# Head norms of two token tiles taken together in a decoder layer's projection, with new numbers in its planner

## The chip, the cores and the metric

The kernel runs on one core of a Trainium2 chip. The metric is the device time of one execution in microseconds (us), taken as the median of the runs shown. One execution was also recorded by the profiler. TensorE (PE in the profile; its weight loads are PEld) multiplies matrices and transposes, VectorE (DVE) and ScalarE (ACT) do elementwise work, and SyncE (SP) issues nearly all DMAs. A matmul writes into PSUM, which is handed out here as banks of 128 x 512 floats.

## The reference, cut to what matters

One layer of a decoder trunk: a half-step SwiGLU feed-forward, an RMS norm, one wide projection `u @ W_in`, three attentions, a gated merge through `W_out`, and a second half-step feed-forward. 1024 tokens, model width 1024, all in float32.

```python
h = x + 0.5 * swiglu(rmsnorm(x, g1), ...)
u = rmsnorm(h, g)
z = u @ W_in                      # fox q,k,v,f | dsa q,k,v | indexer q,k,w | mem q | gates
fq, fk = head_norm(fq), head_norm(fk)      # 8 heads of 64, RMS over each head, then gains
dq     = rope(head_norm(dq))               # 8 heads of 64
o_A = fox_attention(...)          # causal, with log forget gates
o_B = dsa_attention(...)          # each query keeps the top 256 keys by indexer scores
o_C = memory_attention(...)       # 4 heads of 128 over 256 memory tokens
h = h + (sum_i sigmoid(u @ W_g_i) * (o_i @ W_br_i)) @ W_out
y = h + 0.5 * swiglu(rmsnorm(h, g2), ...)
```

(The lines on the three norms of heads stand here in short for what the kernel computes between the projection and the attentions; the two other score products, the masks and the softmaxes are left out.)

## The kernel before, in words

Every large product is made of three TensorE products of split operands (`mm3`): each float32 operand is held as a high part and a rest, and high by high, high by rest and rest by high are summed in PSUM. ACT makes the high part of a weight (`wH`), DVE the rest (`wL`). Tokens come in 8 tiles of 128.

The program runs in this order: feed-forward 1 (to about 690 us), norm and the narrow columns of the projection, the wide columns of the projection (about 735 to 1108 us), the attentions (to 1698), the last branch product and the product with `W_out`, feed-forward 2.

**The projection.** Six column blocks of 512 run one after the other over the 8 tiles, in the order MQ (memory queries), IQ (indexer queries), FK and FQ (keys and queries of the forgetting attention), FV (its values), DQ (queries of the sparse attention). `Block.step` is one tile of one block: 24 matmuls of 512 columns into one PSUM bank, `tm`, then a `consume` of its own. For MQ, FK, FQ and DQ this is `head_norm`: ACT squares the bank into a tile in SBUF (`hsq`), DVE sums it by heads (`hv`), nine small DVE operations on 128 x 8 values make the reciprocal root (`rs_y`, `rs_a`), and one DVE multiplication writes the normed tile. For DQ a rotation follows (five DVE operations). Then `turn` transposes the tile on PE through another bank, ACT and DVE split it (`th`, `tl`), and SP stores both parts. FV's consume is one split and one store; it has no norm and no turn.

In this stage PSUM is four single banks, shared by `tm`, `turn` and the gate products, and two buffers of two banks each (`banks2`), which the index scores `isc` use. An index score is four matmuls of up to 512 columns into such a double bank (fewer columns for earlier tiles), a ReLU on ACT and a weighted sum on DVE (`acc`). As soon as a tile of queries has its scores, `selection`, a background chain, looks for the threshold of its top 256 keys by bisection, 32 rounds for a tile: ACT counts over the score row (`junk`), DVE makes the next threshold (`sk`, `sn`).

**The planner.** `_Flow` writes the order out when the program is built. It keeps a clock for each engine from a small table of costs; chains of work are generators that yield between steps, each with a time (`c.t`) at which its next step is ready. `fl.run(chains, width, filler, background, pace)` takes the first ready chain of the first `width`, else a step of `filler`, and steps `background` whenever it is due. The compiler's scheduler then orders the instructions of each engine on that basis. In the projection the filler is the gate product (`gates_f`, 96 steps of 12 matmuls); what is left of it, then branch products 2 and 0 (16 steps of 12 each, named `br`), is the filler of the attentions. There `pace()` lets the filler run as far as the heads' share of their steps, plus `PACE` steps, and holds `RESERVE` steps back; `left` (L1751) is the number of filler steps that the heads spread out. Branch 1 has to wait for the last sparse head: `last_branch` stores that head's output, loads it again with the others' (`wS<-o_s`), splits it (`wH` and `wL` in the profile) and runs 192 matmuls.

**The start of the attentions.** `mem_head` issues four loads on SP (`qs`, `vs`, `km`, `vm`), says when its operands are expected (`fl.t = max(fl.t, fl.clk["PE"]) + 4.0`, L1267) and yields; its first matmuls are `spm`. Two heads are open at a time (`width=2`). On SP these loads stand behind the last stores of the sparse queries.

Of the kernel before, what the change touches and what calls it, by code (L numbers as in the profile page):

```python
# [9 lines left out]
F32 = mybir.dt.float32  # L10
# [9 lines left out]
P = 128  # L20
# [132 lines left out]
PACE, RESERVE = 4, 6  # L153


def trunk_layer_kernel(
# [182 lines left out]
    class Block:  # L339
# [13 lines left out]
        def step(self, u, t, consume, after=None):  # L353
# [5 lines left out]
            pt = self.out(t) if self.out else bank("tm")  # L359
            kper = 1024 // self.ncols  # L360
# [7 lines left out]
            yield from consume(t, pt)  # L368
# [8 lines left out]
    def block_chains(blocks, u, nt, deps=None, after=None):  # L377
        cs = []
        for i, (b, consume) in enumerate(blocks):
            nxt = blocks[i + 1][0] if i + 1 < len(blocks) else after  # L380
            order = getattr(consume, "order", range(getattr(consume, "first", 0), nt))
            for t in order:
                cs.append(chain(b.step(u, t, consume, nxt if t == order[-1] else None),
                                deps[t] if deps and i == 0 else getattr(consume, "deps", ())))
# [472 lines left out]
    def head_norm(tp, pt, nh, sq=None):  # L857
        hd = 512 // nh
# [397 lines left out]
    def mem_head(tp, h):  # L1256
# [10 lines left out]
        fl.t = max(fl.t, fl.clk["PE"]) + 4.0  # L1267
# [379 lines left out]
    def normed(dst, nh, scale):  # L1647
        def consume(t, pt):
            xn = head_norm(tp, pt, nh)
            yield  # L1650
            parts = turn(tp, xn, scale)
            if nh == 8:
                store_pairs(dst, t, parts)
            else:
                for i, w in enumerate(parts):
                    store(dst[i].rearrange("h d t -> d h t")[:, :, t * P:(t + 1) * P], w)
        return consume

    def sparse_queries(t, pt):
        xn = head_norm(tp, pt, 8)  # L1660
        o = tp.tile([P, 512], F32, tag="hx", name="hsq", bufs=4)
        bc = lambda a, s: a.unsqueeze(1).to_broadcast(s)
        rotate(tp, o.rearrange("p (h a d) -> p h a d", h=8, a=2), xn.rearrange("p (h a d) -> p h a d", h=8, a=2),
               bc(cgq[:, t], [P, 8, 2, 32]), bc(sgq[:, t, 0], [P, 8, 32]), bc(sgq[:, t, 1], [P, 8, 32]), 8)
        yield
        store_pairs(dq_s, t, turn(tp, o))

    def fox_values(t, pt):
# [6 lines left out]
    blocks = [(mq_block, normed(mq_s, 4, gmx[:, 0:1])), (mk_block(C_IQ), index_queries),  # L1675
              (mk_block(C_FK), normed(fk_s, 8, None)), (mk_block(C_FQ), normed(fq_s, 8, gfx[:, 0:1])),
              (mk_block(C_FV), fox_values), (mk_block(C_DQ), sparse_queries)]
# [73 lines left out]
    left = 2 * 24 * 2 - gates_f.n + 40  # L1751
# [121 lines left out]
```

## Time and profile before

| | us |
|---|---|
| median of 3 runs | 2497.53 |
| fastest and slowest run | 2496.92 and 2503.78 |
| the profiled execution | 2504.25 |
| its span, first to last instruction | 2502.2 |
| PE busy in that span | 2412.6 (96%) |
| DVE and ACT busy | 1617.9 (65%) and 1149.1 (46%) |
| mean granted TensorE clock | 0.984 of full speed |

The busy shares are means over stages with different limits, so the profile is read stage by stage: a table of windows gives the length of a stage, each engine's busy time in it and the clock that TensorE was granted; the table of waits says what an idle PE waited for; the timeline shows single instructions with the idle time before them; and the chain of waits shows what led to the work that ended last.

### The profile page before, as it was taken

The page shows a single profiled execution, that of the slowest core. Times are in us where ns is not written, and L with a number is a line of the kernel's source. Part 1 is how long each engine was busy: PE and PEld are TensorE (multiplying, and loading weights), DVE is VectorE, ACT ScalarE, POOL GpSimd, SP SyncE. Part 2 cuts the span into 40 slices and gives each one's busy share as a digit, 9 for nine tenths or more (in the row PEclk, how much of TensorE's full clock was granted, in tenths as well). Part 3 has the DMA queues.
Part 4 walks back from the last instruction along what each step waited for, and adds up shares of the span by engine and source line. Part 5 has one row for each costly group of instructions (what it writes and reads, how often), then busy time and mean ns, then how long its engine had stood idle before and what let it go on. Part 6 is the DMA issues. An engine that isn't in the chain of part 4 may idle for free.

```text
span 2502.2 us, 31494 instructions
## 1 busy us (share of the span) xinstructions
PE 2412.6 (96%) x11532; PEld 1995.0 (80%) x11532; DVE 1617.9 (65%) x3162; ACT 1149.1 (46%) x1918; POOL 2.2 (0%) x40
## 2 busy tenths in 40 slices
PE   6999999999999999989999999998999999999999
PEld 5888888888788877777787888887877888888887
DVE  7755555478767588685564556777367555554885
ACT  6443333343443376768864555543144333333332
POOL 0000000000000000000000000000000000000000
PEclk8999999999999999999999999999999999999999
DMA  4333322484445534544554546667413222225643
GB/s 136 117 103 110 101 92 73 146 316 142 135 131 146 163 100 137 164 147 137 153 162 135 154 133 195 194 200 238 145 64 93 85 93 76 84 93 194 260 151 131
DMA packets 300922, 352.15 MB, mean 141 GB/s; under 512 B 19896, under 2 KB 202840, under 8 KB 300768
## 3 DMA queue, kind: packets, MB, share of 16 engines
q1 hardware_dynamic: 300768, 350.15, 43.7%
q8 instruction: 90, 1.47, 0.2%
q14 instruction: 64, 0.52, 0.1%
HBM read 255.51 MB, written 93.54 MB: 139 GB/s over the span
## 4 chain that ended last, share of the span: by engine, by line
PE 74%; DVE 12%; ACT 7%; DMA 4%; issue 3%; SPq 0%; ACTq 0%; DVEq 0%
PE gx L51 19%; PE gy L51 14%; PE dx L51 8%; PE gate L51 7%; PE tm L51 7%; PE dy L51 6%; PE br L51 4%; ACT junk L51 3%; PE po L51 2%; PE sp L51 2%; DVE wL L51 2%; PE pT L51 2%; DMA wS<-in_ffn_w_down 1%; PE nar L51 1%; ACT ns L51 1%
## 5 line engine op out<-in xcount | busy, mean ns | idle before, releaser
L51 ACT CAST wH<-wS 128x1024 fp32r<-128x1024 f32 (+1 forms) x218 | 204.6, 944 | 260.7 <-PE gy L51 78.0
L51 PE MATMUL tm<-wH,u 128*128 128x512 f32 x992 | 319.5, 396 | 3.4 <-ACT wH L51 3.4
L51 DVE TENSOR_TENSOR wL<-wS,wH 128x1024 fp32r<-128x1024 f32 (+1 forms) x218 | 236.2, 1089 | 101.1 <-ACT wH L51 98.8
L51 PE MATMUL gate<-u,wH 128*128 128x512 f32 x768 | 248.9, 401 | 0.0
L51 PE MATMUL gx<-th,wH 128*128 128x512 f32 x704 | 223.2, 399 | 10.3 <-ACT wH L51 6.2
L51 PE MATMUL gy<-th,wH 128*128 128x512 f32 x704 | 220.9, 395 | 5.3 <-DVE th L51 3.5
L51 PEld LDWEIGHTS tm<-wH,u 128*128 128x128 f32 x992 | 187.4, 189 | 42.0 <-ACT wH L51 4.6
L51 PE MATMUL gx<-raw,wH 128*128 128x512 f32 x704 | 216.9, 389 | 0.4 <-DVE gu L51 0.4
L51 PE MATMUL tm<-wL,u 128*128 128x512 f32 x496 | 195.1, 393 | 1.0 <-DVE wL L51 0.8
L51 ACT ACTIVATE junk<-wk,sn 128x384 bf16<-128x384 f32 (+5 forms) x186 | 164.3, 883 | 67.4 <-DVE sn L51 59.0
L51 PEld LDWEIGHTS gx<-th,wH 128*128 128x128 f32 x704 | 135.0, 193 | 40.6 <-ACT wH L51 7.4
L51 ACT CAST wH<-S 128x1024 fp32r<-128x1024 f32 x88 | 92.2, 1051 | 157.9 <-PE gy L51 149.9
L51 PEld LDWEIGHTS gy<-th,wH 128*128 128x128 f32 x704 | 133.6, 190 | 34.7 <-DVE th L51 4.4
L51 PEld LDWEIGHTS gate<-u,wH 128*128 128x128 f32 x768 | 140.3, 191 | 24.8 <-DVE u L51 0.2
L51 DVE TENSOR_TENSOR pl<-pT,ph 128x512 fp32r<-128x512 f32 (+1 forms) x176 | 110.1, 639 | 74.5 <-ACT ph L51 73.1
L51 DVE TENSOR_TENSOR wL<-S,wH 128x1024 fp32r<-128x1024 f32 x88 | 107.4, 1223 | 75.1 <-ACT wH L51 75.1
L51 DVE TENSOR_TENSOR gu<-gu,gy 128x512 f32<-128x512 f32 x88 | 60.3, 686 | 147.0 <-PE gy L51 104.1
L51 PEld LDWEIGHTS gx<-raw,wH 128*128 128x128 f32 x704 | 132.0, 188 | 28.2 <-DVE gu L51 0.8
L51 PE MATMUL gate<-u,wL 128*128 128x512 f32 x384 | 151.7, 395 | 0.0
L51 PE MATMUL dx<-wH 128*128 128x512 f32 x352 | 138.4, 393 | 2.7 <-DVE rows L51 2.6
L51 PE MATMUL gx<-th,wL 128*128 128x512 f32 x352 | 139.1, 396 | 0.6 <-DVE wL L51 0.5
L51 PE MATMUL gy<-th,wL 128*128 128x512 f32 x352 | 138.8, 394 | 0.0
(270 smaller groups left out, 5018.1 us busy)
## 6 DMA issues: line engine op xcount, KB each, us to landing
wS<-in_ffn_w_down SPq DMA_DIRECT2D x70, 512.0 KB
wS<-in_w_in SPq DMA_DIRECT2D x48, 512.0 KB
wS<-in_ffn_w_gate SPq DMA_DIRECT2D x46, 512.0 KB
wS<-in_ffn_w_up SPq DMA_DIRECT2D x44, 512.0 KB
hid_s<-gu SPq DMA_DIRECT2D x44, 512.0 KB
a<-hid_s SPq DMA_DIRECT2D x30, 512.0 KB
g_s<-sg SPq DMA_DIRECT2D x48, 256.0 KB
bg<-g_s SPq DMA_DIRECT2D x48, 256.0 KB
```

What stands on the lines that cost most here:

```text
L51: return fn(*a, **k)
```

## The change

Four edits.

1. The norm of heads for FK, FQ and DQ takes two tiles at once. `Block.pair` makes both tiles' products (2 x 24 matmuls) into the two halves of one double bank, from the same two buffers that the index scores use, and `pair_norm` runs one norm over 128 x 1024. Turns, rotations and stores stay one for each tile. MQ keeps its norm of one tile.
2. FV moves from fifth place to third: MQ, IQ, FV, FK, FQ, DQ.
3. `PACE` goes from 4 to 8, and the constant in `left` from 40 to 37: the filler may run 8 steps ahead of the heads, and 3 steps more of it are kept for after them.
4. Memory heads 0 and 1 expect their operands 12.0 instead of 4.0 after PE's clock.

```diff
-PACE, RESERVE = 4, 6
+PACE, RESERVE = 8, 6
...
+        def pair(self, u, t, consume, after=None):
+            self.fetch()
+            if fl.clk["PE"] < self.ready[0]:
+                yield self.ready[0]
+            pt = banks2("tm")
+            self.product(pt[:, :512], u, t, None)
+            yield 0.0
+            if after is not None:
+                after.fetch(self.bufs - len(self.srcs))
+            self.product(pt[:, 512:], u, t + 1, after)
+            yield from consume(t, pt)
...
-        fl.t = max(fl.t, fl.clk["PE"]) + 4.0
+        fl.t = max(fl.t, fl.clk["PE"]) + (12.0 if h < 2 else 4.0)
...
+    def pair_norm(pt):
+        return head_norm(tp, pt, 16, tp.tile([P, 1024], F32, tag="hp", name="hsq", bufs=2))
+
+    def normed_pair(dst, scale):
+        def consume(t, pt):
+            xn = pair_norm(pt)
+            for i in range(2):
+                yield
+                store_pairs(dst, t + i, turn(tp, xn[:, i * 512:(i + 1) * 512], scale))
+        return in_pairs(consume)
...
+    @in_pairs
+    def sparse_queries(t0, pt):
+        xn = pair_norm(pt)
...
+        for i in range(2):
+            yield max(os_[i][1], fl.t if i else 0.0)
+            store_pairs(dq_s, t0 + i, turn(tp, os_[i][0]))
...
-              (mk_block(C_FK), normed(fk_s, 8, None)), (mk_block(C_FQ), normed(fq_s, 8, gfx[:, 0:1])),
-              (mk_block(C_FV), fox_values), (mk_block(C_DQ), sparse_queries)]
+    blocks = [(mq_block, memory_queries), (mk_block(C_IQ), index_queries), (mk_block(C_FV), fox_values),
+              (mk_block(C_FK), normed_pair(fk_s, None)), (mk_block(C_FQ), normed_pair(fq_s, gfx[:, 0:1])),
+              (mk_block(C_DQ), sparse_queries)]
...
-    left = 2 * 24 * 2 - gates_f.n + 40
+    left = 2 * 24 * 2 - gates_f.n + 37
```

By the count of the two programs the change takes 132 instructions from DVE (the eleven of a norm, twelve times) and 12 from ACT. PE has 11532 matmuls, and SP 942 DMAs, in both. The rows of both programs are the same on PE up to the middle of the indexer's queries (about 867 us in the trace). Three places behind that, on PE.

**The first pair.** Before, the index scores of the later tiles lie among tiles of FK, each tile with a bank of its own; `tm_7203` and `tm_7281` are such tiles, `isc_...` the scores, `gate_...` the filler. Only the first matmul of each run of one tile is shown.

```order
L51 MATMUL tm_7203<-wH_6558,u1_4704 128x512
...
L51 MATMUL isc_6895<-ikk0_5380,iqs_6625 128x512
...
L51 MATMUL isc_6902<-ikk0_5380,iqs_6806 128x512
...
L51 MATMUL tm_7203<-wH_6558,u1_4704 128x512
L51 MATMUL gate_6771<-u1_4704,wH_6015 128x512 x2
L51 MATMUL isc_6958<-ikk0_5380,iqs_6806 128x512
...
L51 MATMUL gate_6771<-u1_4704,wH_6015 128x512
L51 MATMUL turn_7264<-ident_69,hsq_7156 128x128 x4
L51 MATMUL tm_7281<-wH_6521,u1_4704 128x512
...
L51 MATMUL isc_6969<-ikk0_5380,iqs_6965 128x512
...
L51 MATMUL isc_7034<-ikk0_5380,iqs_6806 128x512
...
L51 MATMUL tm_7281<-wH_6521,u1_4704 128x512
```

After, at the first pair of FK (`tm_7132`, 48 matmuls in one double bank; `tm_7251` is the next pair):

```order
L51 MATMUL tm_7132<-wH_7098,u0_4703 128x512
L51 MATMUL isc_7169<-ikk0_5380,iqs_6846 128x512
...
L51 MATMUL tm_7132<-wH_7061,u0_4703 128x512
...
L51 MATMUL isc_7179<-ikk0_5380,iqs_6950 128x512
...
L51 MATMUL tm_7132<-wH_7074,u0_4703 128x512
...
L51 MATMUL isc_7189<-ikk0_5380,iqs_6846 128x512
...
L51 MATMUL tm_7132<-wH_7098,u0_4703 128x512
...
L51 MATMUL isc_7244<-ikk0_5380,iqs_6950 128x512
...
L51 MATMUL tm_7251<-wH_7061,u0_4703 128x512
...
L51 MATMUL isc_7282<-ikk0_5380,iqs_6950 128x512
...
L51 MATMUL turn_7292<-ident_69,hsq_7220 128x128 x4
L51 MATMUL tm_7251<-wH_7061,u0_4703 128x512
```

Ahead of these rows seven scores now stand in one run, with no other matmul between them. `tm_7132` holds one of the two double banks up to its norm, so that `isc_7169`, `isc_7179`, `isc_7189` and `isc_7244` follow one another in the other one, which `tm_7251` then takes; `isc_7189` and `isc_7244` have three matmuls between them. Before, the two buffers went from score to score.

**The end of the projection.** From the last `tm` (DQ's last tile) over the turns of the sparse queries to the first memory head's `spm`. Before:

```order
L51 MATMUL tm<-wH,u_4704 128x512
L51 MATMUL turn<-ident,hsq 128x128 x4
L51 MATMUL gate<-u_4703,wH 128x512 x2
...
L51 MATMUL turn<-ident,hsq 128x128 x4
L51 MATMUL gate<-u_4703,wH 128x512 x2
...
L51 MATMUL turn<-ident,hsq 128x128 x4
L51 MATMUL gate<-u_4703,wH 128x512 x2
...
L51 MATMUL gate<-u_4703,wL 128x512
L51 MATMUL spm<-km,qs 128x256 x2
L51 MATMUL spm<-km,vs 128x256
```

After:

```order
L51 MATMUL tm<-wH,u_4704 128x512
L51 MATMUL turn<-ident,hsq 128x128 x8
L51 MATMUL gate<-u_4704,wH 128x512 x2
...
L51 MATMUL gate<-u_4704,wL 128x512
L51 MATMUL turn<-ident,hsq 128x128 x4
L51 MATMUL gate<-u_4703,wH 128x512 x2
...
L51 MATMUL gate<-u_4703,wL 128x512
L51 MATMUL turn<-ident,hsq 128x128 x8
L51 MATMUL gate<-u_4703,wH 128x512 x2
...
L51 MATMUL gate<-u_4704,wL 128x512
L51 MATMUL spm<-km,qs 128x256 x2
L51 MATMUL spm<-km,vs 128x256
```

Between the last `turn` and `spm` stood 24 gate matmuls, and stand 72 now. Before, three turns stood behind the last `tm`, 12 gate matmuls between each two. Now two turns follow it at once (the first `x8`), then 24 gate matmuls and the turn of the last pair's first tile (the lone `x4`), and after 12 more the last two turns, the second of them of the last pair's other tile.

**The end of the attentions.** `po` is the last sparse head's product with its values; `br` with `o_14311` (before) and `o_14107` (after) is the filler, `br` with the other `o_` the final branch, 12 matmuls for each number. Before:

```order
L51 MATMUL po_15239<-ph_15344,vs_12666 128x128
L51 MATMUL po_15239<-pl_15345,vs_12666 128x256
...
L51 MATMUL br_15388<-o_14311,wH_14600 128x512
...
L51 MATMUL br_15408<-o_14311,wH_14600 128x512 x2
...
L51 MATMUL br_15446<-o_14429,wH_15426 128x512 x2
...
L51 MATMUL br_15467<-o_14429,wH_15426 128x512 x2
...
L51 MATMUL br_15488<-o_14429,wH_15426 128x512 x2
```

After:

```order
L51 MATMUL po_14979<-ph_15072,vs_12477 128x128
L51 MATMUL po_14979<-pl_15073,vs_12477 128x256
...
L51 MATMUL br_15124<-o_14107,wL_14249 128x512
...
L51 MATMUL br_15144<-o_14107,wH_14396 128x512 x2
...
L51 MATMUL br_15164<-o_14107,wH_14396 128x512 x2
...
L51 MATMUL br_15184<-o_14107,wH_14396 128x512 x2
...
L51 MATMUL br_15204<-o_14107,wH_14396 128x512 x2
...
L51 MATMUL br_15242<-o_14225,wH_15222 128x512 x2
```

Behind the last `po` two filler steps (24 matmuls, one of them ahead of it) were left before the final branch; five are left now (60, two ahead). These 36 matmuls are gone from among the heads: the stretch ahead of the last `po` that has no filler in it was 126 matmuls long and is 162.

## Rows read from the trace of the kernel before

**Rows 1.** The page's first part, busy us and share by engine.

```profile
PE 2412.6 (96%) x11532; PEld 1995.0 (80%) x11532; DVE 1617.9 (65%) x3162; ACT 1149.1 (46%) x1918; POOL 2.2 (0%) x40
```

**Rows 2.** Stages: us, busy us of PE, PEld, DVE, ACT, POOL, clock, DMA.

```profile
867.00:1108.50 241.50, 229.24 (x1036) 184.89 (x1034) 192.01 (x682) 174.47 (x358) 0.00 (x0) 0.98 0.43 129
1108.50:1124.00 15.50, 8.05 (x39) 6.51 (x38) 10.96 (x36) 9.24 (x20) 0.00 (x0) 0.85 0.92 308
1124.00:1250.00 126.00, 118.06 (x656) 96.70 (x656) 70.16 (x227) 109.09 (x242) 0.00 (x0) 0.98 0.48 148
1250.00:1698.40 448.40, 438.11 (x2550) 371.32 (x2549) 292.13 (x672) 239.37 (x482) 0.00 (x0) 1.00 0.56 166
1698.40:1757.30 58.90, 52.04 (x217) 42.07 (x216) 42.52 (x58) 17.97 (x24) 0.00 (x0) 0.91 0.79 265
```

**Rows 3.** The same table for four shorter stretches.

```profile
930.00:1000.00 70.00, 64.33 (x286) 52.23 (x285) 58.78 (x202) 49.40 (x98) 0.00 (x0) 0.95 0.43 133
1119.50:1126.30 6.80, 3.88 (x14) 3.17 (x13) 2.03 (x10) 5.38 (x13) 0.00 (x0) 0.50 1.01 355
1675.00:1698.40 23.40, 22.64 (x155) 19.94 (x155) 21.08 (x45) 13.07 (x25) 0.00 (x0) 1.00 0.44 136
1706.60:1716.80 10.20, 6.18 (x14) 4.42 (x15) 6.33 (x6) 4.08 (x4) 0.00 (x0) 0.50 1.01 370
```

**Rows 4.** PE's waits from 867 to 1108.5: total us, times, longest.

```profile
PE turn L51 <- DVE hsq L51: 3.9, 2, 3.0
PE isc L51 <- DVE acc L51: 3.8, 3, 1.9
...
PE turn L51 <- DVE sk L51: 1.0, 1, 1.0
```

**Rows 5.** DVE's groups by shape from 867 to 1108.5: busy us, mean ns, idle before.

```profile
L51 DVE TENSOR_TENSOR wL<-wS,wH 128x1024 fp32r<-128x1024 f32 x14 | 17.1, 1224 | 3.4 <-ACT wH L51 3.1
L51 DVE TENSOR_TENSOR hsq<-tm,rs_y 128x512 f32<-128x512 f32 x24 | 16.6, 691 | 0.3
L51 DVE TENSOR_REDUCE hv<-hsq 128x8 f32<-128x512 f32 x24 | 16.4, 685 | 2.8 <-ACT hsq L51 1.4
...
L51 DVE SCALAR_TENSOR_TENSOR acc<-isc,iw,acc 128x1024 f32<-128x1024 f32 x7 | 9.0, 1280 | 1.7 <-ACT isc L51 1.7
...
L51 DVE SCALAR_TENSOR_TENSOR rs_y<-rs_a,rs_y 128x8 f32<-128x8 f32 x48 | 8.0, 166 | 0.9
```

**Rows 6.** ACT's groups by shape, the same stretch.

```profile
L51 ACT ACTIVATE hsq<-tm 128x512 f32<-128x512 f32 x24 | 14.1, 586 | 6.3 <-DVE sk L51 3.2 <-PE tm L51 3.1
...
L51 ACT ACTIVATE isc<-isc 128x1024 f32<-128x1024 f32 x8 | 8.0, 1006 | 2.2 <-PE isc L51 2.1
```

**Rows 7.** ACT's timeline, the last rotated query tile: start, us.

```profile
1101.03 0.60 ACT L51 ACTIVATE hsq<-tm 128x512 f32<-128x512 f32 x1 [0.30 <-DVE sk L51]
```

**Rows 8.** PE's timeline, last turn, first memory head: start, us, [idle before].

```profile
1108.17 0.63 PE L51 MATMUL turn<-ident,hsq 128*128 128x128 f32 x4 [0.99 <-DVE sk L51]
...
1118.80 0.48 PE L51 MATMUL spm<-km,qs 128*128 128x256 f32 x2 [4.53 <-DMA km<-km_s]
...
1122.79 0.77 PE L51 MATMUL spm<-km,qs 128*128 128x256 f32 x2 [2.92 <-DMA km<-km_s]
```

**Rows 9.** PE's waits from 1108.5 to 1698.

```profile
PE pT L51 <- ACT ns L51: 8.2, 9, 1.9
```

**Rows 10.** PE's timeline, the last filler matmul and the final branch's first.

```profile
1703.37 0.39 PE L51 MATMUL br<-o,wL 128*128 128x512 f32 x1
1710.38 1.22 PE L51 MATMUL br<-o,wH 128*128 128x512 f32 x2 [6.63 <-ACT wH L51]
```

**Rows 11.** The chain of waits at the end of attention: start, us.

```profile
1698.51 0.59 ACT lo L51
...
1711.83 45.67 PE br L51 x190
1757.50 2.72 PE tm L51 x12
```

More of the change, by code (lines that the diff above doesn't have):

```diff
@@ L380, in block_chains @@
             nxt = blocks[i + 1][0] if i + 1 < len(blocks) else after
-            order = getattr(consume, "order", range(getattr(consume, "first", 0), nt))
+            pair = getattr(consume, "pair", False)
+            order = range(getattr(consume, "first", 0), nt, 2 if pair else 1)
             for t in order:
-                cs.append(chain(b.step(u, t, consume, nxt if t == order[-1] else None),
+                cs.append(chain((b.pair if pair else b.step)(u, t, consume, nxt if t == order[-1] else None),
                                 deps[t] if deps and i == 0 else getattr(consume, "deps", ())))
@@ L1645, in trunk_layer_kernel, with in_pairs, memory_queries @@
     sel_c = chain(selection())
-    def normed(dst, nh, scale):
-        def consume(t, pt):
[L1649 to L1661, printed above, removed]
-        bc = lambda a, s: a.unsqueeze(1).to_broadcast(s)
[L1663 to L1666, printed above, removed]
+    def in_pairs(consume):
+        consume.pair = True
+        return consume
+    def pair_norm(pt):
+        return head_norm(tp, pt, 16, tp.tile([P, 1024], F32, tag="hp", name="hsq", bufs=2))
+    def normed_pair(dst, scale):
+        def consume(t, pt):
+            xn = pair_norm(pt)
[3 more added lines that the diff above has]
+        return in_pairs(consume)
+    def memory_queries(t, pt):
+        xn = head_norm(tp, pt, 4)
+        yield
+        for i, w in enumerate(turn(tp, xn, gmx[:, 0:1])):
+            store(mq_s[i].rearrange("h d t -> d h t")[:, :, t * P:(t + 1) * P], w)
+    @in_pairs
+    def sparse_queries(t0, pt):
+        xn = pair_norm(pt)
+        bc = lambda a, s: a.unsqueeze(1).to_broadcast(s)
+        os_ = []
+        for i in range(2):
+            t = t0 + i
+            o = tp.tile([P, 512], F32, tag="hx", name="hsq", bufs=4)
+            rotate(tp, o.rearrange("p (h a d) -> p h a d", h=8, a=2),
+                   xn[:, i * 512:(i + 1) * 512].rearrange("p (h a d) -> p h a d", h=8, a=2),
+                   bc(cgq[:, t], [P, 8, 2, 32]), bc(sgq[:, t, 0], [P, 8, 32]), bc(sgq[:, t, 1], [P, 8, 32]), 8)
+            os_.append((o, fl.t))
+        for i in range(2):
+            yield max(os_[i][1], fl.t if i else 0.0)
+            store_pairs(dq_s, t0 + i, turn(tp, os_[i][0]))
     def fox_values(t, pt):
```

7 lines of the change are left out of this document (4 added, 3 removed).

## Prediction, made before the changed kernel ran

> **What bounds the kernel now.** The page's first part comes first: PE is busy for 2412.6 us, 96% of the span, DVE for 65% and ACT for 46% [rows 1]. PE's work stays the same matmul for matmul, so the change can win only what PE loses: time in which it idles, and time at half clock. The table by stages shows where that lies in the part of the program that the change touches [rows 2]. From 867 to 1108.5 PE is busy for 229.24 of 241.5 us and idles for 12.3; a mean granted clock of 0.98 costs about 0.02 x 241.5 = 4.8 more. The 15.5 us around the start of the attentions hold only 8.05 us of PE work. From 1124 to 1250, where ACT is busy for 109.09 of 126 us, PE idles for 7.9 and loses about 2.5 to the clock. The main part of the attentions, 1250 to 1698.4, has 10.3 us of idle time in 448.4. The stage behind it loses 6.9 us of 58.9 to idling, and its clock is 0.91.
>
> Then the waits by name. Inside the projection they are few and short: turns for the normed tile 3.9 us and for a step of the selection 1.0, scores for `acc` 3.8 [rows 4]. One stretch holds much of it: 930 to 1000, PE 64.33 of 70 us at clock 0.95, DVE busy for 58.78 [rows 3]; its idle time and its half clock make 5.7 + 3.5 = 9.2 us. At the start of the attentions PE waits twice for `km`, 4.53 and 2.92 us [rows 8]. At the end one wait of 6.63 us for `wH` stands between the last filler matmul and the final branch [rows 10]. Behind each of the two last places the clock is at its half level, 1.2 instead of 2.4 GHz (0.50): 3.88 us of PE work in the stretch of 6.8 us, and 6.18 in that of 10.2 [rows 3]; half of that work's time, 1.9 and 3.1 us, is lost. So PE bounds every stage, and the prizes are single places: up to 17 us in the projection, 9.3 at the start of the attentions, 10.4 behind it, 9.7 at the end.
>
> **One: the norms in pairs.** A pair replaces two sets of eleven DVE operations by one. The nine small ones cost 166 ns each at 128 x 8 [rows 5]; at 128 x 16 I take the same, so a pair saves 9 x 0.166 = 1.5 us. The two multiplications cost 2 x 0.691; one of 1024 columns is taken as the subtraction of that width, 1.224 [rows 5], and saves 0.16. The sum by heads, 2 x 0.685, has no row at 1024 columns; between 1.224 and `acc`'s 1.280 it saves 0.1. Together 1.8 us for a pair and 21 for twelve, out of 192.01 [rows 2, 5]. On ACT 2 x 0.586 against a wide operation like the score's ReLU, 1.006 [rows 6], saves 0.17 for a pair, 2 us in all. None of this is on the path as such, since PE bounds the stage. It pays where PE waits for DVE, above all in 930 to 1000. I let it, together with FV's tiles (which have no norm) among the scores, remove some 12 of the 17 us.
>
> Against it stand waits that the new order makes. First, the run of seven scores. A score is four matmuls, 4 x 0.227 = 0.91 us (the rows of the output product give 2.72 us for twelve of 512 columns [rows 11]); DVE needs 1.280 for its sum [rows 5]. With two buffers, five of the seven wait for DVE: 5 x (1.28 - 0.91) = 1.9 us if DVE did nothing else, and 5 x (1.28 / 0.8 - 0.91) = 3.5 if it gives them the 80% that the stage leaves it busy for; with the clock behind it I take 4. Second, the scores that share one buffer. Such a round is 0.91 on PE, 1.006 on ACT and 1.280 on DVE, so that the next score waits 2.29 us less what stands between: three matmuls (0.7) between the third and the fourth, which leaves 1.6; nothing ahead of the second pair, which leaves 2.3; a turn ahead of the third pair, 0.6 [rows 8], which leaves 1.7. That is 5.6 us. One more for turns of the first pairs and one for the clock make 11.6. Net of this part: **-12 + 11.6, with -1 us** as the round number. Bounds: all 17 won and 8 paid is -9; half of it won and twice the serial waits paid is +10.
>
> FV's move adds no instruction. Its work (one split, one store for each tile) was hidden under PE in its old place, where PE was idle for nothing, and is in the new one by the same cover.
>
> **Two: the last pair of DQ.** Before, the last tile's norm begins at 1101.03 [rows 7] and its turn runs at 1108.17 behind a wait of 0.99 [rows 8]: a chain of 7.1 us under 24 gate matmuls and two turns. For a pair the square is 0.42 longer, the sum by heads 0.6, the multiplication 0.53, and DVE has another split and another rotation product of 512 columns in the row (2 x 0.69, as `hsq` [rows 5]): 10.0 us to the first turn. PE has two turns and 24 gate matmuls for it, 1.2 + 24 x 0.227 = 6.6. So a new wait of 3.4 us, with about 1.5 for the clock behind it; 0 if DVE is early here, 5.5 + 2 if the selection's steps get in between.
>
> Here is a rule that speaks against the change. DVE is busy for 80% of the stage and ACT for 72%, yet PE waits for them [rows 2, 4]. The Trainium skill, "Perfetto Trace Analysis", section "Optimizing Scalar/DVE Operations", says that grouping helps where such an engine is saturated, and that where it isn't, but causes bubbles on others, breaking instructions up may let work complete sooner. By the rows the pair's tail costs 4.9 us once, at the one place where no next block stands behind it; by the rule every pair would show it. I go by the rows for the sum, and keep the rule's case as a rival.
>
> **Three: 12.0 instead of 4.0.** The loads stand behind the same stores on SP's queue as before. The first `spm` came 10.6 us behind the last turn and the second head's 14.6 [rows 8]. 72 gate matmuls instead of 24 now cover 72 x 0.227 = 16.3 us from the last turn. Both waits go (-7.4), and the half clock behind them (-1.9). With the +4.9 of part two: -4.4, **-4 us** for the start of the attentions. Bounds -9 (no new wait) and +3 (loads that arrive 5 us later, as their stores do, and a wait that stays).
>
> **Four: 8 steps ahead.** From 1124 to 1250 PE waits beside a busy ACT, mostly transposes for the probabilities: 8.2 us in 9 waits up to 1698 [rows 9]. More filler in that stretch covers such waits; the rows of the changed program put only 12 more gate matmuls between the first memory head and the first sparse product. Between 0 and all of 10.4 us I take **-2**, near the low end for so few.
>
> **Five: three more steps for the end.** Behind the last `po` 23 filler matmuls are left before, 58 after. From the sums of the last head to the final branch's rest of the weights lie 1711.83 - 1698.51 = 13.3 us [rows 11]; 58 x 0.227 = 13.2 now cover it, so 6.63 falls to nearly nothing, and the half clock (3.1) with it: -9.5. The three steps are missing among the heads instead. The unfilled stretch before cost little: PE 22.64 of 23.4 us [rows 3], 3%; on 36 x 0.227 = 8.2 us that is 0.3. If nothing else covered them it would be 8.2. I take +1, by the row of the same stretch: **-8.5**, with -9.5 and -1.5 as bounds. Next late there would be the DMA of the reloaded outputs, which the chain holds already.
>
> **The sum.** -1 - 4 - 2 - 8.5 = -15.5 us. The profiled execution took 2504.25 us, 6.7 above the median, with a span of 2502.2; against its own time the change gives 2488.8. The median was 2497.53, so the forecast is 2482.
>
> **Rivals.** *The projection shortens too:* the new waits hide behind the order's slack, since scores and pairs are spread further apart on the chip than the rows' neighbours suggest, and part one gives -13 instead of -1: 2470. For it, 21 us less of DVE in a stage where it is busy for 80%; against it, that PE is idle for only 12.3 us there [rows 2].
>
> *The gain is eaten:* part one at its bound of +10, or the loads late and the end's chain as late as before; the rest stays: -15.5 + 11, about 2493, within 0.3%.
>
> *Slower:* the pairs' tails bind. A pair needs a whole double bank from its first matmul to its wide multiplication; its norm takes 1.0 + 1.28 + 9 x 0.2 + 1.22 = 5.3 us behind its product. Two such banks exist, and scores want them too. Where a pair finds both taken, PE waits up to 5.3 us and runs on at half clock for some time (as 1.5 above): nearly 7. With the other parts as forecast (-14.5), against these and the 12 us that part one wins it decides from four such pairs (26.5 / 7 = 3.8), and at five of twelve 5 x 7 - 26.5 is +8.5, 2506. It is the case of the Trainium skill's rule above. Against it: with no score in between, the other bank's product of 48 matmuls lasts 48 x 0.227 = 10.9 us, twice the norm.
>
> *The change doesn't do what it says:* the filler is kept, but the chain at the end starts later or its loads take longer, and the 6.63 stay in part. That is 2485 to 2490, inside the forecast.
>
> **How the numbers follow.** Forecast (2474 to 2489) 0.50; projection shorter too (below 2474) 0.17; eaten 0.20; slower 0.13. About 0.3%, 7.5 us, is what a measurement of this kernel can tell from no change, so faster is 0.67, same 0.20, slower 0.13. The range leaves out the slower case and the far end of the shorter one: 2464 to 2500.
>
> **What would show it.** Right: no wait for `km` over 1 us, no wait over 1 us for `wH` ahead of the final branch and no clock of 0.50 there; DVE's busy time in the projection down by about 20 us; one wait of some 4 us at the turn of DQ's last pair; waits of scores and of `tm` for `acc` of 8 to 12 us in FK's first pairs. Wrong: waits of `tm` for `hsq` at several pairs (the slower case), an end that still waits, or a projection whose length differs by more than 10 us.

## The result, and the profile after

The change made the kernel slower: 2520.47 us against 2498.04 measured beside it, a ratio of 1.0085 with a 95% interval of 1.0063 to 1.0107. The profiled execution of the changed kernel has a span of 2520.0 us, 17.8 more than the one before; the medians differ by 22.4, since the profiled execution before took 2504.25 us, 6.2 above the median.

To see where the 17.8 us arose, both traces are cut at the same places of the program, and the filler is taken out of each stage: the stage's length in the timeline less 0.2267 us (the twelfth part of 2.72, [rows 11]) for each filler matmul in it, and for the final branch's 192 matmuls ahead of the output product. What is left is comparable, since the other work of a stage is the same. Differences are taken before rounding.

| stage, without its filler (us) | before | after | difference |
|---|---|---|---|
| first score to last `tm` of DQ | 248.7 | 263.2 | +14.6 |
| to the first `spm` | 7.5 | 9.5 | +2.0 |
| to the last `po` | 290.9 | 298.1 | +7.2 |
| to the first `tm` of the output product | 10.3 | 4.5 | -5.8 |
| to the end | 744.8 | 747.1 | +2.2 |
| ahead of the first score (untouched) | 808.2 | 805.8 | -2.4 |

The table by stages of the changed kernel (us, busy us of PE, PEld, DVE, ACT, POOL, clock, DMA share, GB/s), cut at 985, at DQ's last `tm`, the first `spm` and the last `po`; then two rows of the kernel before, cut at 985 too:

```profile
867.00:985.00 118.00, 100.58 (x417) 77.97 (x416) 76.04 (x227) 83.21 (x178) 0.00 (x0) 0.94 0.34 107
985.00:1107.40 122.40, 118.52 (x546) 95.99 (x545) 88.72 (x292) 80.33 (x151) 0.00 (x0) 0.99 0.44 128
1107.40:1141.20 33.80, 29.25 (x130) 24.08 (x129) 23.32 (x71) 20.47 (x38) 0.00 (x0) 0.90 0.65 211
1141.20:1711.90 570.70, 544.13 (x3144) 459.64 (x3143) 358.66 (x889) 344.91 (x719) 0.00 (x0) 0.98 0.52 159
```

```profile
867.00:985.00 118.00, 113.64 (x524) 91.58 (x522) 96.38 (x330) 88.95 (x189) 0.00 (x0) 0.99 0.42 129
985.00:1108.50 123.50, 115.61 (x513) 93.31 (x512) 95.63 (x353) 85.52 (x170) 0.00 (x0) 0.97 0.44 128
```

Up to 985 us, where FV's tiles, the scores and FK's first two pairs lie, PE idles for 17.4 of 118 us and has a clock of 0.94. From there to the last `tm` it loses only 3.9 us and one hundredth of the clock. Before, it was the other way round: 4.4 us and one hundredth up to 985, 7.9 and three hundredths behind. The heads have a clock of 0.98; before, it was 0.98 only up to 1250 and 1.00 behind [rows 2].

PE's waits in the projection (us in total, times, longest), to be read beside [rows 4], where scores waited 3.8 us for `acc` and `tm` never did:

```profile
PE isc L51 <- DVE acc L51: 7.3, 4, 2.6
PE tm L51 <- DVE acc L51: 5.1, 2, 2.7
PE isc L51 <- DVE sk L51: 4.3, 4, 1.4
...
PE turn L51 <- DVE hsq L51: 1.1, 1, 1.1
```

Three of them on PE's timeline, and the clock behind one (two matmuls of 512 columns take 1.05 us instead of about 0.62):

```profile
960.34 1.15 PE L51 MATMUL isc<-ikk,iqs 128*128 128x512 f32 x4 [2.06 <-DVE acc L51]
963.91 0.79 PE L51 MATMUL tm<-wH,u 128*128 128x512 f32 x1 [2.42 <-DVE acc L51]
...
964.93 1.05 PE L51 MATMUL tm<-wH,u 128*128 128x512 f32 x2
...
983.26 0.71 PE L51 MATMUL tm<-wH,u 128*128 128x512 f32 x1 [2.72 <-DVE acc L51]
```

The sizes that the prediction took for the wide operations hold, row by row. DVE's groups by shape from 867 to 1125, answering to [rows 5] (busy us, mean ns, idle before), and ACT's, answering to [rows 6]:

```profile
L51 DVE TENSOR_TENSOR hsq<-tm,rs_y 128x1024 f32<-128x1024 f32 x12 | 14.7, 1223 | 0.1
L51 DVE TENSOR_REDUCE hv<-hsq 128x16 f32<-128x1024 f32 x12 | 14.6, 1219 | 6.0 <-ACT hsq L51 6.0
...
L51 DVE SCALAR_TENSOR_TENSOR rs_y<-rs_a,rs_y 128x16 f32<-128x16 f32 x24 | 4.2, 174 | 0.5
```

```profile
L51 ACT ACTIVATE hsq<-tm 128x1024 f32<-128x1024 f32 x12 | 12.1, 1012 | 1.8 <-PE tm L51 1.7
```

The engines' busy time over the whole program fell by less than these rows add up to, on DVE from 1617.9 [rows 1] to 1604.9 us, 13.0 less:

```profile
PE 2418.1 (96%) x11532; PEld 1999.2 (79%) x11532; DVE 1604.9 (64%) x3030; ACT 1148.0 (46%) x1906; POOL 2.2 (0%) x40
```

At the start of the attentions the two waits for `km` [rows 8] are gone, and the turn of DQ's last pair waits instead:

```profile
1118.46 1.09 PE L51 MATMUL turn<-ident,hsq 128*128 128x128 f32 x4 [4.55 <-DVE hsq L51]
```

Among the heads the waits grew. Before, from 1108.5 to 1698, transposes waited 8.2 us [rows 9], and products with the values:

```profile
PE po L51 <- DVE pl L51: 3.5, 5, 1.0
PE po L51 <- ACT ph L51: 2.8, 4, 1.3
```

PE's waits in the changed kernel from 1125 to 1712:

```profile
PE pT L51 <- ACT ns L51: 10.3, 10, 2.3
PE po L51 <- ACT ph L51: 6.0, 6, 1.5
PE po L51 <- DVE pl L51: 5.9, 9, 1.4
PE sp L51 <- DMA ks<-fk_s: 3.2, 1, 3.2
```

At the end the wait for `wH` fell from 6.63 [rows 10] to 2.7, and one of the output product is new:

```profile
PE br L51 <- ACT wH L51: 2.7, 1, 2.7
PE tm L51 <- DVE wL L51: 2.1, 1, 2.1
```

### The profile page after: what moved, and what is told of

It is laid out like the page before. It is cut to its first block, busy times and chain, and to the rows that moved or that the text cites. A ratio compares the mean times of both kernels' runs of the same rounds, so it can differ in the third digit from the quotient of the medians.

```text
span 2520.0 us, 31339 instructions
## 1 busy us (share of the span) xinstructions
PE 2418.1 (96%) x11532; PEld 1999.2 (79%) x11532; DVE 1604.9 (64%) x3030; ACT 1148.0 (46%) x1906; POOL 2.2 (0%) x40
## 4 chain that ended last, share of the span: by engine, by line
PE 71%; DVE 11%; DMA 6%; ACT 6%; issue 4%; SPq 0%; ACTq 0%; DVEq 0%
PE gx L51 19%; PE gy L51 14%; PE dx L51 7%; PE gate L51 7%; PE tm L51 7%; PE dy L51 6%; ACT junk L51 3%; PE po L51 2%; DVE wL L51 2%; PE pT L51 2%; PE br L51 2%; PE sp L51 2%; DMA wS<-in_ffn_w_down 2%; DMA bg<-g_s 1%; DMA wS<-in_w_in 1%
## 5 line engine op out<-in xcount | busy, mean ns | idle before, releaser
L51 PE MATMUL gx<-th,wH 128*128 128x512 f32 x704 | 222.5, 398 | 10.3 <-ACT wH L51 6.2
```

The lines of the kernel that those rows point to most:

```text
L51: return fn(*a, **k)
```

## The experiments

Three theories of the loss in the projection and among the heads were set against one another. A1: the first pairs and the scores share two double banks. A2: FV's place alone lets scores run one behind another. B and its followers: the three numbers cost time among the heads. In the tables, us is the median, ratio is to the kernel before, measured in the same rounds (its median was 2498.0 to 2501.0); stages are those of the first table, without filler, of the profiled execution. A profiled execution can lie some us beside the median (pairs_sb_fv5_old's span was 2508.4), much of it in stages that no edit touches: the last one, to the end, lies between 741.2 and 749.4 us in the kernels with all stores on SP. The first stage is steadier: in the nine of them with the order of the kernel before in it (the kernel before and eight with new numbers alone) it takes 247.1 to 251.3 us.

**The parts of the change alone.**

```diff
numbers_only: the kernel before, with
-PACE, RESERVE = 4, 6
+PACE, RESERVE = 8, 6
-        fl.t = max(fl.t, fl.clk["PE"]) + 4.0
+        fl.t = max(fl.t, fl.clk["PE"]) + (12.0 if h < 2 else 4.0)
-    left = 2 * 24 * 2 - gates_f.n + 40
+    left = 2 * 24 * 2 - gates_f.n + 37
fv_only: the kernel before, with FV third in blocks
fk_single: the changed kernel, with a fox_keys(t, pt) of one tile in place of normed_pair(fk_s, None)
fv_fifth: the changed kernel, with FV fifth in blocks
```

> The kernel before with the three new numbers alone (PACE 8, left 37, operands of memory heads 0 and 1 expected 12.0 later); no pairs, FV in fifth place. Theory A (the numbers are worth what the prediction gave them; pairs and FV's place cost the time): both km waits (7.4 us) and 6 us or more of the end are gone, the heads lose 1 to 2, so 10 to 15 us faster than before, near 2485. Rival B (the filler kept back costs among the heads what it wins at the end, and loads for the first forgetting head come late): the stretch from the first spm to the last po is 8 to 12 us longer for equal work, so within 4 us of before, 2494 to 2500.

> The kernel before with FV in third place alone; single norms, old numbers. Theory A1 (the first pairs and the scores share the two double banks, and that makes the waits): without pairs the projection keeps its length within 4 us, 2494 to 2502. Rival A2 (FV's place alone lets seven to nine scores run one behind another, each waiting for acc): scores wait for DVE for 10 us or more between 910 and 960 and the time rises by 8 to 14 us, 2506 to 2512.

> The changed kernel with FK's norms one tile at a time; FQ and DQ in pairs, FV third, new numbers. The last scores then lie among single tiles of FK. Theory A1 (sharing of the double banks by the first pairs and scores): the waits of tm and isc for acc in the first pairs go, the projection is 10 us or more shorter than with all three in pairs, about 2506. Rival A2 (FV's place): the run of scores stays and so does its cost, 2514 to 2520. Under both one wait of 4 to 5 us stays at the turn of DQ's last pair.

> The changed kernel with FV back in fifth place; pairs and new numbers stay. Nine scores then run one behind another ahead of FK's first pair, and later ones between the pairs. Theory A1 (pairs and scores share the double banks): more scores meet pairs than with FV third, so the projection is as long or longer by up to 10 us, 2518 to 2530. Rival A2 (FV's place alone): the time falls by 8 us or more, 2506 to 2512.

| | us | ratio (95%) | score to last `tm` | to `spm` | to last `po` | to output product |
|---|---|---|---|---|---|---|
| before | 2500 | 1 | 248.7 | 7.5 | 290.9 | 10.3 |
| after | 2520.5 | 1.0085 (1.0063 to 1.0107) | 263.2 | 9.5 | 298.1 | 4.5 |
| numbers_only | 2508.5 | 1.0033 (1.0020 to 1.0045) | 249.1 | 2.8 | 306.2 | 4.1 |
| fv_only | 2505.4 | 1.0018 (1.0010 to 1.0027) | 257.3 | 8.8 | 287.9 | 10.7 |
| fk_single | 2514.2 | 1.0061 (1.0045 to 1.0077) | 251.0 | 8.7 | 302.5 | 2.1 |
| fv_fifth | 2551.6 | 1.0209 (1.0196 to 1.0222) | 297.7 | 3.9 | 296.7 | 7.7 |

Neither the numbers nor FV's place gains by itself; the pairs by themselves, in double banks and with the old numbers, were not run. With all other things as in the changed kernel, FK's pairs cost 12.2 us of the projection (263.2 - 251.0), and where FV stands fifth and more scores meet FK's pairs, 34.5 more, far beyond the 10 that A1 had expected. The time of fk_single stayed 8 us above A1's 2506, since its heads take 302.5 us. PE's waits of fv_fifth from 867 to 1143:

```profile
PE isc L51 <- DVE acc L51: 14.0, 7, 2.4
PE isc L51 <- DMA iqs<-iq_s: 5.9, 1, 5.9
PE tm L51 <- DVE acc L51: 5.6, 2, 3.2
```

That speaks for A1, though 5.9 us of fv_fifth's waits are one late load of `iqs`. A2 holds beside it for a part: FV's place alone costs 8.6 us in that stage, but not by the run of scores, whose waits are 6.9 us, in place of 4.2 before, where A2 expected 10 or more. The waits of fv_only there, the longest of them on PE's timeline, and DVE's timeline ahead of it:

```profile
PE turn L51 <- DVE one L51: 6.2, 1, 6.2
PE isc L51 <- DVE acc L51: 4.4, 6, 1.5
```

```profile
1052.76 1.09 PE L51 MATMUL turn<-ident,hsq 128*128 128x128 f32 x4 [6.15 <-DVE one L51]
```

```profile
1045.44 1.48 DVE L51 TENSOR_TENSOR_SCAN wk<-one,sq 128x640 f32<-128x640 f32 x1
1046.84 0.14 DVE L51 SCALAR_TENSOR_TENSOR rs_a<-rs_y 128x8 f32<-128x8 f32 x1
1046.90 1.22 DVE L51 TENSOR_TENSOR wL<-wS,wH 128x1024 fp32r<-128x1024 f32 x1
1048.04 0.16 DVE L51 TENSOR_TENSOR rs_a<-rs_a,hv 128x8 f32<-128x8 f32 x1
1048.11 1.22 DVE L51 TENSOR_TENSOR wL<-wS,wH 128x1024 fp32r<-128x1024 f32 x1
```

The turn that waits 6.2 us needs a norm whose small steps (`rs_a`) stand between the end of one selection (a scan of 1.48 us) and two weight subtractions of 1.22. What else comes due on DVE beside a norm decides its wait, and FV's move changed that. The numbers alone lose nothing in the projection and 15.3 us among the heads: rival B, and more than the 8 to 12 that it expected.

**The scores' banks, taken away as a cause.**

```diff
pairs_single_banks: the changed kernel, with
-            pt = banks2("tm")
-            self.product(pt[:, :512], u, t, None)
+            pt = [bank("tm"), bank("tm")]
+            self.product(pt[0], u, t, None)
...
+        for i in range(2):
+            A.activation(sq[:, i * 512:(i + 1) * 512], pt[i], AF.Square)
pairs_sb_fv5_old: the same, with FV fifth and the old numbers
fq_dq_pairs: pairs in double banks for FQ and DQ alone; FK single, FV fifth, old numbers
```

> The changed kernel with the two products of a pair in two single banks instead of one double bank; the squares and the two multiplications are then one for each tile, the sum by heads and the nine small operations stay one for the pair (1.6 us less DVE work for a pair than two single norms). Scores have the two double banks to themselves. Theory A1 (sharing of the double banks is what the first pairs pay): no tm waits for acc, and the stretch from the first score to the last tm is 8 to 12 us shorter than in the changed kernel, 263 to about 253 for equal filler; 2508 to 2513. Rival A2 (scores in one run are slow whatever banks the pairs have): it stays within 4 us, 2517 to 2524.

> The kernel before with pairs in two single banks; FV fifth, old numbers. Eight to nine scores run in a row inside FK's last tiles, but none waits for a pair's bank. If DVE's relief is worth what the prediction gave it (up to 12 us of waits in the projection), it shows here: the stretch from the first score to the last tm 5 to 10 us shorter than before's 248.7, 2491 to 2497 less what DQ's last pair costs (3 to 5), so 2494 to 2500. Rival (pairs delay the first turn of each and batch the scores, so waits only move): 250 to 262 for that stretch, 2503 to 2515.

> The kernel before with the norms of FQ and DQ in pairs; FK single, FV fifth, old numbers. No score stands beside a pair. From the two runs with FV third, one with these pairs and one without, the pairs of FQ and DQ shorten the projection by about 6 us. Theory A1 (a pair pays where no score wants its banks): the projection is 5 to 8 us shorter, the turn of DQ's last pair waits 4 to 5 us, and the time is 2493 to 2499. Rival (the gain was FV's place under the pairs): no shorter projection, 2500 to 2508.

| | us | ratio (95%) | score to last `tm` | to `spm` | to last `po` |
|---|---|---|---|---|---|
| pairs_single_banks | 2522.9 | 1.0083 (1.0070 to 1.0096) | 262.1 | 5.0 | 304.5 |
| pairs_sb_fv5_old | 2518.4 | 1.0067 (1.0049 to 1.0085) | 254.8 | 9.0 | 297.3 |
| fq_dq_pairs | 2526.7 | 1.0094 (1.0074 to 1.0115) | 257.3 | 9.4 | 305.5 |

PE's waits of pairs_single_banks from 867 to 1108:

```profile
PE tm L51 <- DVE tl L51: 7.3, 2, 4.6
PE isc L51 <- DVE sk L51: 4.9, 6, 1.5
PE turn L51 <- ACT junk L51: 4.6, 2, 3.8
PE isc L51 <- DVE acc L51: 3.0, 4, 1.1
```

As A1 expected, no `tm` waits for `acc` any more, and the scores' waits fall from 11.6 us (7.3 + 4.3) to 7.9. But the stage keeps its length, 262.1 us, where A1 expected about 253: two of the four single banks are now held by a pair, and `tm` waits 7.3 us for a bank that a turn still holds (`tl`), turns 4.6 more. So the double banks explain the waits at the first pairs, and are not a repair: a pair holds two banks from its first product to its norm, wherever they are. (This is read from the waits; no run gives the pairs banks of their own.) That is the point at which A1, read as "the double banks are the cost", falls. In fq_dq_pairs FQ's first pair still met the last two scores, contrary to its expectation, and the stage lost 8.6 us. The 6.3 us that the pairs of FQ and DQ seemed to gain between fv_only and fk_single did not come back here. They are of the size of the 6.2 us wait above, which FV's move had made and which fk_single's trace no longer has; that they are the same is inferred from this alone.

**The numbers one by one.**

```diff
pace_only: PACE 8. kept_only: left + 37. arrival_and_pace: PACE 8 and 12.0. Each in the kernel before.
numbers_fox12, ap_fox12: numbers_only and arrival_and_pace, with
-            return (*r, fl.clk["PE"] + 4.0)
+            return (*r, fl.clk["PE"] + (12.0 if h < 2 else 4.0))
```

> The kernel before with PACE 8 alone. The order up to the first spm is unchanged, so both km waits stay; the heads have four filler steps more to spend early. The prediction's term for this is -2 (between 0 and -10), 2490 to 2500. Rival (filler spent early is missing later among the heads): the stretch from the first spm to the last po is 3 to 8 us longer, 2501 to 2507.

> The kernel before with left 37 alone: three filler steps more behind the last po. Theory B1 (the steps kept for the end are what the heads miss): the wait ahead of the final branch falls from 6.6 to about 2, the heads lose 8 to 12 us, the weights of the output product come 2 us late; 2502 to 2508. Rival B2 (the four steps spent ahead of the first spm are what the heads miss): the end wins 6, the output product gives back 2, the heads lose 3 at most; 2494 to 2499.

> The kernel before with PACE 8 and the operands of memory heads 0 and 1 expected 12.0 later; left stays 40. With all three numbers the stretch from the last product of the projection to the first spm was 4.8 us shorter for equal filler, and the one from the first spm to the last po 15.3 us longer. Theory B1 (the steps kept for the end are what the heads miss): the start stays 4 to 5 us shorter, the heads lose 5 us at most, 2495 to 2500. Rival B2 (the four steps spent ahead of the first spm are what the heads miss): the heads still lose 10 us or more and 2504 to 2509 comes out.

> The kernel before with the three new numbers, and the operands of the first two forgetting heads also expected 12.0 instead of 4.0 later. Theory C1 (in all runs with new numbers the heads lose most of their time at the first forgetting head, whose keys are loaded late behind the memory heads' stores): the wait of sp for ks (4.8 us with the three numbers alone) and the one behind it go, and the first spm to the last po take 5 to 10 us less than with the three numbers, 2499 to 2504. Rival C2 (the filler moved away from the heads is missing anywhere): the waits move to other places and the time stays within 3 us, 2506 to 2511.

> The kernel before with PACE 8 and the operands of both the first two memory heads and the first two forgetting heads expected 12.0 later; left stays 40. Theory C1 (late keys of the first forgetting heads): with PACE 8 and the memory heads' number alone sp waited 1.7, 5.3 and 0.8 us for ks and a transpose 5.9 behind it; these go and the start's gain of 4.8 us stays, 2494 to 2500. Rival C2: 2507 to 2512 as without it.

| | us | ratio (95%) | to `spm` | to last `po` | to output product | to the end |
|---|---|---|---|---|---|---|
| before | 2500 | 1 | 7.5 | 290.9 | 10.3 | 744.8 |
| pace_only | 2519.9 | 1.0072 (1.0057 to 1.0087) | 7.8 | 306.8 | 9.3 | 743.9 |
| kept_only | 2510.7 | 1.0043 (1.0027 to 1.0059) | 7.7 | 302.1 | 6.6 | 744.6 |
| arrival_and_pace | 2510.1 | 1.0037 (1.0023 to 1.0050) | 2.8 | 302.3 | 12.4 | 747.3 |
| numbers_fox12 | 2507.1 | 1.0030 (1.0019 to 1.0041) | 4.6 | 304.1 | 2.0 | 749.4 |
| ap_fox12 | 2512.5 | 1.0036 (1.0023 to 1.0049) | 2.9 | 299.3 | 12.7 | 746.3 |

PACE 8 alone is the worst, beyond its rival's 2507, and kept_only is slow too: each of the two costs 11 to 16 us among the heads. So both the steps kept for the end (B1) and the steps spent ahead (B2) are missing there; the two losses do not add up, since all three numbers together cost 15.3. Where it goes is seen in the 60 us from the first product of scores of a forgetting head (`sp`). Before, and pace_only, same columns as above:

```profile
1208.30:1268.30 60.00, 56.67 (x319) 46.28 (x318) 35.28 (x117) 53.04 (x105) 0.00 (x0) 0.97 0.53 150
```

```profile
1220.40:1280.40 60.00, 43.90 (x229) 35.00 (x228) 35.34 (x106) 41.55 (x82) 0.00 (x0) 0.86 0.37 103
```

319 and 229 matmuls in the same time, at clocks of 0.97 and 0.86. With PACE 8 alone the planner put 264 filler matmuls between the first `spm` and the first `sp` (204 before), and 82 are left in this stretch for 120. What PE lacks there first is the keys. SP's timeline of pace_only, and two of PE's waits:

```profile
1209.21 1.19 SPq L173 DMA_DIRECT2D ks<-fk_s  x2
1214.29 0.33 SPq L176 DMA_DIRECT2D g_s<-sg  x1
1215.26 0.33 SPq L176 DMA_DIRECT2D o_s<-os  x1
1215.68 0.45 SPq L173 DMA_DIRECT2D ks<-fk_s  x1
```

```profile
1228.26 0.76 PE L51 MATMUL sp<-ks,qs 128*128 128x128 f32 x2 [5.32 <-DMA ks<-fk_s]
...
1237.38 0.47 PE L51 MATMUL pT<-ident,ns 128*128 128x128 f32 x1 [5.93 <-ACT ns L51]
```

The key loads stand on SP behind the stores of gates and head outputs (`g_s`, `o_s`), which wait for ACT (8.2 and 9.3 us between 1190 and 1240); PE waits 5.32 us for them and then 5.93 for the softmax, and runs at half clock. Before, more filler lay over the same delay. A later expected arrival for these heads did not move it (C1 fell: the wait stayed at 4.9 us in numbers_fox12).

The same holds beyond the numbers. Over all twenty profiled kernels, the five with 120 or more filler matmuls in the 60 us from the first `sp` take 287.9 to 293.3 us to the last `po`, the fifteen with 82 to 112 take 296.7 to 310.8. Two of the fifteen have the old numbers: fq_dq_pairs (95, and 305.5 us) and pairs_sb_fv5_old (108, and 297.3). Their pairs put 72 gate matmuls ahead of the first `spm` for 48, and PE waits 6.4 and 4.2 us for `ks`. So it is not the numbers as such that cost, but whatever leaves less filler there; which of the fifteen is slower, the count does not tell.

**SP's order or ACT's load.** Stores of gates, masks, head outputs, row sums and merged branches go to GpSimd's queue; loads stay on SP.

```diff
+    def late_store(o, i):
+        nc.gpsimd.dma_start(plain(o), plain(i))
-                    store(g_s[d][:, sl], sg)
+                    late_store(g_s[d][:, sl], sg)
```

> The kernel before with the stores of gates, masks, memory and head outputs, row sums and merged branches issued by GpSimd instead of SP; loads stay on SP. Theory D1 (loads of the next head stand on SP behind stores that wait for ACT): even here the first forgetting head's keys come earlier and the 1.8 us wait of sp goes; 2494 to 2500. Rival D2 (ACT, busy with the selection, sets this stretch whatever the queue): no change within 4 us, or slower if GpSimd issues DMAs more slowly.

> The same move of the stores on the kernel before with the three new numbers alone. D1: the 4.8 us wait of sp for ks and the half clock behind it go, the final branch's weights no longer stand behind the stores of merged branches, and the first spm to the last po take 7 to 12 us less for equal filler than the 306 with the numbers alone; 2490 to 2498. D2: the wait for ks turns into waits of transposes for ACT, 302 to 308 for that stretch and 2504 to 2510.

> The same move on the changed kernel. The projection keeps its loss of about 15 us (pairs and FV's place), whose waits are PE's for DVE. D1: the heads win 5 to 8 us, 2510 to 2516. D2: 2517 to 2524.

> PACE 8 and the memory heads' 12.0 with the same move of the stores, left 40. D1: the waits of sp for ks (1.7, 5.3 and 0.8) and the 5.9 behind them go, 10 us or more; the end keeps its wait of 7; 2496 to 2502. D2: 2506 to 2512.

They took 2508.5, 2515.8, 2526.7 and 2527.1 us, ratios of 1.0037 (1.0023 to 1.0050), 1.0067 (1.0054 to 1.0079), 1.0108 (1.0094 to 1.0121) and 1.0106 (1.0089 to 1.0123): all slower than with SP alone. With the numbers, the key loads now follow one another on SP and the wait for them falls from 4.8 to 2.2 us, but the stage to the last `po` stays at 305.3 us for 306.2. SP's row, and PE's waits from 1126 to 1704:

```profile
1204.72 6.11 SPq L173 DMA_DIRECT2D ks<-fk_s  x4
```

```profile
PE pT L51 <- ACT ns L51: 11.6, 9, 3.2
PE po L51 <- DVE pl L51: 7.5, 9, 1.6
...
PE sp L51 <- DMA ks<-fk_s: 2.2, 1, 2.2
```

So D1 names the wait for the keys rightly, and D2 the stage: the waits of transposes and value products for ACT and DVE (softmax, splits) stay, 25.2 us for 25.1. Three of the four times lie above D2's range too, so the move has a cost of its own.

**Smaller steps of the same numbers.**

```diff
arrival8: the kernel before, with
+        fl.t = max(fl.t, fl.clk["PE"]) + (8.0 if h < 2 else 4.0)
arrival12_pace5: 12.0, and PACE 5
```

> The kernel before with the operands of memory heads 0 and 1 expected 8.0 instead of 4.0 later; PACE 4, left 40. The planner puts 13 gate matmuls (2.9 us) more ahead of the first spm. Theory E (filler spent where a wait is certain is won, filler spent further ahead is missing at the first forgetting heads): the first km wait falls from 4.5 to about 1.6, the heads lose 2 us at most, 2494 to 2499. Rival (any shift ahead of the first forgetting head costs there): heads 5 us longer or more, 2501 to 2508.

> The kernel before with the memory heads' 12.0 and PACE 5; left 40. 36 gate matmuls more stand ahead of the first spm, as with PACE 8. Theory E: both km waits go (start 4.8 us shorter), and with only one step of lead more the first forgetting heads keep their filler; the heads lose 5 us at most, 2495 to 2501. Rival: the heads lose 10 us or more, as with PACE 8, 2504 to 2510.

| | us | ratio (95%) | to `spm` | to last `po` | to output product |
|---|---|---|---|---|---|
| arrival8 | 2498.8 | 0.9987 (0.9978 to 0.9997) | 4.1 | 289.7 | 9.2 |
| arrival12_pace5 | 2499.5 | 0.9994 (0.9985 to 1.0004) | 2.8 | 292.7 | 10.4 |

Theory E holds. arrival8 is the only version that beats the kernel before, by 0.13%, with an interval that stops just short of 1 (0.9997); what speaks for it is the place: 13 gate matmuls moved to where PE waited for `km` anyway, and the stage to `spm` is 3.4 us shorter. Its waits there, 1108 to 1125:

```profile
PE spm L51 <- ACT sg L51: 1.2, 1, 1.2
...
PE spm L51 <- DMA km<-km_s: 0.3, 1, 0.3
```

With 12.0 and PACE 5 the start is as short as with PACE 8, and the stretch from the first `sp` is whole again, 316 matmuls:

```profile
1203.80:1263.80 60.00, 56.05 (x316) 45.67 (x314) 35.23 (x119) 53.06 (x105) 0.00 (x0) 0.97 0.54 152
```

## Why the prediction was wrong

The forecast was -15.5 us; the profiled span rose by 17.8 and the median by 22.4. Its prices for single waits were mostly good; what it took to be covered was not.

- **DVE's and ACT's relief: right by the rows, too large for the engines.** 1.223, 1.219 and nine of about 0.174 us make 4.0 for a pair where two norms took 5.7; 1.7 instead of 1.8. But DVE's busy time fell by 13.0 us and not by 21: a row often begins before the one ahead of it has ended, so that lengths of rows add up to more than the time they take. ACT's 1148.0 us lie among the 1147.7 to 1149.6 of ten kernels with single norms; of the 2 us nothing is to be seen.
- **The gain in the projection, "-12": the step that failed first.** I let 12 of the stage's 17 lost us vanish because DVE was busy for 80%. The waits were few and each had a cause of its own (a bank, a selection's end, a weight). In the changed kernel 24.5 us are lost up to 985 (17.4 idle, 7.1 by the clock), more than the 17 of the whole stage before, and 5.1 from there on. Before, the two stretches lost 5.5 and 11.6: behind 985 some 6.5 us did go, about half of the 12, and ahead of it 19.0 came. The whole stage is 14.6 us longer without its filler, beyond the bound of +10. Pairs without FV's move and without double banks gained nothing either (254.8). The sum has slips besides: -12 + 11.6 is -0.4, not -1, and its upper bound comes to +8.7 (17.2 paid, 8.5 won), not +10.
- **The new waits, "+11.6": right places, too small.** The three serial waits came as worked out: 2.06, 2.42 and 2.72 us for 1.6, 2.3 and 1.7. The run of seven scores cost 7.5 (four waits between 926 and 941) for 4: the sum gave the scores 80% of DVE, but that share was all of DVE's work, and two of the four waits ended with a step of the selection (`sk`). The clock was taken as 1 us; in the 118 us up to 985 it cost 0.06 x 118 = 7.
- **FV's move, "nothing": wrong.** It costs 8.6 us alone, most of it one wait of 6.2 that what then fell due on DVE made.
- **DQ's last pair: right.** 4.55 us for 3.4, inside its bound. The rule of the Trainium skill ("Perfetto Trace Analysis", "Optimizing Scalar/DVE Operations") is borne out here, and only here as a wait for the longer norm: in the rest of the projection one turn waited for `hsq`, 1.1 us. What the pairs cost elsewhere was, by the waits, the banks held.
- **12.0: right at its place.** Both `km` waits went, 7.4 us. With the numbers alone the stage to the first `spm` is 2.8 us for 7.5; with the pairs it is 9.5, so that DQ's last pair took 6.7 there for the 4.9 of the sum.
- **"8 steps ahead, -2" and the "+1" for the filler kept back: the second step that failed.** The heads are 7.2 us longer, though they start without 2.9 us of waiting. I priced the missing filler by the idle share of one unfilled stretch (3%, [rows 3]), where the keys of the first forgetting heads set another price. numbers_only shows it without any pair: +15.3; fq_dq_pairs shows +14.6 without any of the numbers, since its pairs take filler from the same place.
- **The end, "-8.5": half.** The 6.63 fell to 2.7 and not to nothing, and the output product waits 2.1 for weights. What was late next is on the chain of waits of the changed kernel behind the last `po` (start, us):

```profile
1715.82 3.46 DMA mg_s<-bg
...
1720.23 6.56 DMA wS<-in_w_branch
```

The final branch's weights (`wS<-in_w_branch`) stand on SP behind the store of the filler's branch, which waits for DVE. The chain that I had timed ended at the reloaded outputs.

- **The rivals.** "Slower" came, with half of its mechanism: pairs found banks taken, by scores at two pairs and not by norms at five. A loss among the heads was no rival of mine, and it is the larger part of what the numbers did.

What stays open: how the 7 to 16 us among the heads divide between the late keys and ACT's load. The runs show both, and that neither a later expected arrival nor another queue for the stores brings them back. In the projection it stays open whether pairs with banks of their own would gain.

## What to carry to other kernels

A filler is a stock: spend it only where a wait is certain, and look at the place that it is taken from, since the next late operand decides the price there and not the average idle share. Take an engine's relief from its busy time, not from a sum of row lengths. Before joining two tiles into one operation, count how long the pair holds its PSUM banks and who else uses them; the saved instructions pay only if the engine that they leave was what the next product waited for. In a kernel whose order was set by hand, change one number at a time and in small steps: 8.0 gained 0.13% where 12.0 with a longer lead lost 0.4%.

## What the runs showed of the hardware

- Moving 146 stores from SP's queue to GpSimd's made each of four versions slower by 0.2 to 0.7%, although in numbers_pool_stores the loads behind them went out earlier. In the kernel before the projection grew from 248.7 to 253.1 us, in the changed kernel it did not (262.3 for 263.2); through which path the cost came was not traced.
- Behind waits of 2.06 and 2.42 us the granted clock was 0.50 from 964 to 968 in the changed kernel, 1.2 GHz instead of 2.4. The 13 matmuls from 963.91 to 969.62 took 5.7 us, where 13 x 0.2267 is 2.9: about 2.8 us lost beside 4.5 of waiting. From 940 to 944, amid the waits of the seven scores, it was 0.50 too.
- Rows of DVE overlap: `rs_a` at 1046.84 above takes 0.14 us, and `wL` begins at 1046.90. In the changed kernel the lengths of all DVE rows add up to 20.8 us less than before, the time in which DVE is busy to 13.0 less.
